# Row maximum of a 32 x 512 x 1024 array: two blocks of rows become one long block and a last row in two halves

## The chip, the cores and the metric

The kernel runs on one core of a Trainium2 chip. The metric is device time in microseconds. Before the change it is 165.11 us, the median of three runs (165.09 to 165.19).

Four parts of the core take part. The SyncE queue (SP) issues the loads, VectorE (DVE) reduces, the ScalarE queue (ACT) issues the stores, and 16 DMA engines move the bytes of both queues. TensorE does nothing.

## The reference

The input is `x`, 32 x 512 x 1024 numbers of 4 bytes, 67.11 MB. The output is the maximum over the last axis, 16,384 numbers.

```python
def reference(x: np.ndarray) -> np.ndarray:
    return np.max(x, axis=-1).astype(np.float32)
```

Every byte of `x` has to be read once and compared once; almost nothing is written.

## The kernel before, in words

The first two axes are flattened to 16,384 rows of 1024 numbers. With 128 partitions that makes 128 rows per partition.

The rows are cut into two blocks. In the first block, 112 x 128 rows, partition p holds rows 112p to 112p + 111; in the second, 16 x 128 rows, it holds 16 rows in the same way. A load takes some rows of every partition, 4 KB each, and these lie next to each other in memory within a partition. The list `BLOCKS` (line 13) gives the rows per partition of each load: it begins with loads of 14 and ends with loads of 1, 15 loads in the first block and 11 in the second.

The loads go into `ring`, a buffer of 46 rows per partition. A load takes the next free rows, and starts again at row 0 when it would run past the end. Line 49 issues the load on the SP queue. Line 50 has VectorE reduce it, with one maximum per row written to its column of `res` (128 partitions x 128 columns). After each block, line 54 issues a store of the block's columns on the ACT queue. A partition's results are adjacent in the output: pieces of 448 bytes in the first block and of 64 bytes in the second.

The framework adds the waits. A reduce waits for its load; a load waits until the reduces of the rows that it overwrites are done, and until the semaphore that it is to use is free, of which there are eight for all transfers; a store waits for its block's last reduce. Each queue issues in its own order, so what waits at its head holds up what is behind it. There is no planner with costs or due times.

Of the kernel before, what the change touches and what calls it, by code (L numbers as in the profile page):

```python
# [1 line left out]

# [4 lines left out]


F32 = mybir.dt.float32

BLOCKS = [
    [14, 14, 12, 11, 9, 8, 8, 7, 6, 5, 4, 4, 4, 3, 3],
    [2, 2, 2, 2, 2, 1, 1, 1, 1, 1, 1],
]
RING = 46


@with_exitstack  # L20
def kernel(
    ctx: ExitStack,
    tc: tile.TileContext,
    x: bass.AP,
    out: bass.AP,
):
    nc = tc.nc
    P = 128
    X = mybir.AxisListType.X

    xf = x.flatten_outer_dims()
    N, D = xf.shape
    I = N // P
    of = out.flatten_outer_dims()

    once = ctx.enter_context(tc.tile_pool(name="once", bufs=1))
    ring = once.tile([P, RING, D], F32)
    res = once.tile([P, I], F32)

    at = first = 0  # L40
    for loads in BLOCKS:
        S = sum(loads)
        xb = xf[first * P:(first + S) * P, :].rearrange("(p i) d -> p i d", p=P)
        b = 0
        for g in loads:
            if at + g > RING:
                at = 0
            xc = ring[:, at:at + g, :]
            nc.sync.dma_start(out=xc, in_=xb[:, b:b + g, :])  # L49
            nc.vector.reduce_max(out=res[:, first + b:first + b + g], in_=xc, axis=X)  # L50
            at += g
            b += g
        dst = bass.AP(tensor=of.tensor, offset=of.offset + first * P, ap=[[S, P], [1, S]])
        nc.scalar.dma_start(out=dst, in_=res[:, first:first + S])
        first += S
    assert first == I


# [1 line left out]
_INS = ['x']  # L60
_OUTS = [((32, 512), 'float32')]


# [23 lines left out]
```

## Time and profile before

| what | value |
|---|---|
| median of the runs | 165.11 us |
| the profiled execution: time | 165.1 us |
| the profiled execution: span | 163.3 us |
| VectorE busy | 138.5 us in 26 reduces (85%) |
| VectorE idle, waiting for a load | 22.4 us in 4 waits, the first of 20.1 us |
| read from memory | 67.11 MB, 411 GB/s over the span |
| mean duration of a reduce of one row | 1208 ns |
| mean duration of a reduce of 14 rows | 15086 ns |
| last store, from issue to landing | 1.4 us |

The span is the stretch between the first and the last instruction that the profiler recorded. Times within it count from its start. A line of the profile that names a group of instructions gives the source line, the engine and the operation, then what is written and read with shapes, how often, the busy time with the mean of one in ns, and the idle time ahead of it with what ended it. The chain that ended last is followed back from the last instruction, at each step to what released it. A line of a stretch gives its length, then each engine's busy time, the clock granted to TensorE, the busy share of the 16 DMA engines and the rate in GB/s.

### The profile page before, as it was taken

What the parts mean: (1) busy time and instruction counts of PE and PEld (TensorE: products, weight loads), DVE (VectorE), ACT (ScalarE), POOL (GpSimd) and SP (SyncE); (2) the same over time, 40 slices, a digit from 0 to 9 for tenths busy, and PEclk for the clock granted to TensorE, in tenths of its full rate; (3) what the DMA queues carried; (4) which work ended last, traced back from release to release, by engine and by line L of the source; (5) the groups of instructions that cost most, each with busy time, mean ns of one, the idle gap of its engine ahead of it and who ended that gap; (6) DMA issues with size and microseconds to landing.
All of it is one profiled execution on the core that took longest, in us unless ns stands there. A gap on an engine that the chain in (4) does not pass through costs nothing.

```text
span 163.3 us, 109 instructions
## 1 busy us (share of the span) xinstructions
DVE 138.5 (85%) x26; POOL 0.2 (0%) x4
## 2 busy tenths in 40 slices
DVE  0000099969999999999999999999999999999994
POOL 0000000000000000000000000000000000000000
DMA  6999999998899897999989999999999999999980
GB/s 225 449 449 449 449 449 449 449 417 385 385 409 522 353 530 321 433 433 441 473 385 473 425 449 400 434 395 451 413 425 433 429 414 418 425 421 419 404 357 2
DMA packets 4032, 67.18 MB, mean 411 GB/s; under 512 B 704, under 2 KB 704, under 8 KB 1472
## 3 DMA queue, kind: packets, MB, share of 16 engines
q1 hardware_dynamic: 3744, 67.11, 96.4%
q10 hardware_dynamic: 288, 0.07, 0.2%
HBM read 67.11 MB, written 0.07 MB: 411 GB/s over the span
## 4 chain that ended last, share of the span: by engine, by line
DMA 57%; DVE 40%; DVEq 1%; SPq 0%; issue 0%
DMA ring<-in_x_dram 57%; DVE res L50 40%; DVEq L82 1%; SPq L49 0%
## 5 line engine op out<-in xcount | busy, mean ns | idle before, releaser
L50 DVE TENSOR_REDUCE res<-ring 128x1 f32<-128x1024 f32 (+11 forms) x26 | 138.5, 5396 | 22.4 <-DMA ring<-in_x_dram 22.4
L71 POOL MEMSET const-bfloat16-1.0<- 128x1 bf16 x1 | 0.1, 101 | 0.0
L71 POOL MEMSET const-uint8-127<- 128x1 uint8 x1 | 0.1, 101 | 0.0
L71 POOL MEMSET const-float32-0.0<- 128x1 f32 x1 | 0.1, 98 | 0.2 <-issue 0.2
L71 POOL MEMSET const-float32-1.0<- 128x1 f32 x1 | 0.1, 98 | 0.0
## 6 DMA issues: line engine op xcount, KB each, us to landing
ring<-in_x_dram SPq DMA_DIRECT2D x2, 7168.0 KB, 27.6
ring<-in_x_dram SPq DMA_DIRECT2D x2, 4096.0 KB, 31.6
ring<-in_x_dram SPq DMA_DIRECT2D x1, 6144.0 KB, 49.9
ring<-in_x_dram SPq DMA_DIRECT2D x3, 2048.0 KB, 36.8
ring<-in_x_dram SPq DMA_DIRECT2D x1, 5632.0 KB, 29.7
ring<-in_x_dram SPq DMA_DIRECT2D x5, 1024.0 KB, 24.6
ring<-in_x_dram SPq DMA_DIRECT2D x1, 4608.0 KB, 23.7
ring<-in_x_dram SPq DMA_DIRECT2D x1, 3584.0 KB, 38.4
```

The costliest lines, as they stand in the source:

```text
L50: nc.vector.reduce_max(out=res[:, first + b:first + b + g], in_=xc, axis=X)
L71: nc = _bacc.Bacc("TRN2", target_bir_lowering=False, num_devices=1)
L82: with _tile.TileContext(nc) as tc:
```

## The change

The two blocks become one long block and one last row.

- The long block has 127 rows per partition, so partition p holds rows 127p to 127p + 126. Its 27 loads have the sizes in `ROWS`. The ring holds 45 rows in place of 46.
- The last row of each partition comes from the last 128 rows of the flattened input: partition p takes row 16,256 + p. It is loaded in two halves of 512 numbers (2 KB), the first into the ring, the second into a new buffer `tail` behind a gap of 16 numbers.
- The first store now comes after both of these loads in the program. It waits for the reduce of the 127th row and writes 127 numbers (508 bytes) per partition.
- The first half's maximum is written to the number just ahead of the second half in `tail`. The second reduce runs over that number and the 512 behind it, 513 in all, and so gives the maximum of the whole row. It depends on the first reduce.
- The last store writes one number (4 bytes) per partition; the 128 numbers are adjacent in the output.

```diff
-BLOCKS = [
-    [14, 14, 12, 11, 9, 8, 8, 7, 6, 5, 4, 4, 4, 3, 3],
-    [2, 2, 2, 2, 2, 1, 1, 1, 1, 1, 1],
-]
-RING = 46
+ROWS = [14, 13, 11, 11, 9, 8, 8, 7, 6, 5, 5, 4, 4, 3, 3, 2, 2, 2, 2, 1, 1, 1, 1, 1, 1, 1, 1]
+RING = 45
+RUN = 127
...
+    H = D // 2
...
+    xr = xf[:RUN * P, :].rearrange("(p i) d -> p i d", p=P)
+    out_r = bass.AP(tensor=of.tensor, offset=of.offset, ap=[[RUN, P], [1, RUN]])
...
+        x_last = xf[RUN * P:, :]
+        out_last = bass.AP(tensor=of.tensor, offset=of.offset + RUN * P, ap=[[1, P], [1, 1]])
...
-    at = first = 0
-    for loads in BLOCKS:
-        S = sum(loads)
-        xb = xf[first * P:(first + S) * P, :].rearrange("(p i) d -> p i d", p=P)
-        b = 0
-        for g in loads:
-            if at + g > RING:
-                at = 0
-            xc = ring[:, at:at + g, :]
-            nc.sync.dma_start(out=xc, in_=xb[:, b:b + g, :])
-            nc.vector.reduce_max(out=res[:, first + b:first + b + g], in_=xc, axis=X)
-            at += g
-            b += g
-        dst = bass.AP(tensor=of.tensor, offset=of.offset + first * P, ap=[[S, P], [1, S]])
-        nc.scalar.dma_start(out=dst, in_=res[:, first:first + S])
-        first += S
+    PAD = 16
+    tail = once.tile([P, PAD + H], F32)
+
+    b = at = 0
+    for g in ROWS:
+        if at + g > RING:
+            at = 0
+        xc = ring[:, at:at + g, :]
+        nc.sync.dma_start(out=xc, in_=xr[:, b:b + g, :])
+        nc.vector.reduce_max(out=res[:, b:b + g], in_=xc, axis=X)
+        at += g
+        b += g
+
+    if at + 1 > RING:
+        at = 0
+    half = ring[:, at, :H]
+    nc.sync.dma_start(out=half, in_=x_last[:, :H])
+    nc.sync.dma_start(out=tail[:, PAD:], in_=x_last[:, H:])
+    nc.scalar.dma_start(out=out_r[:, :I - 1], in_=res[:, :I - 1])
+    nc.vector.reduce_max(out=tail[:, PAD - 1:PAD], in_=half, axis=X)
+    nc.vector.reduce_max(out=res[:, I - 1:], in_=tail[:, PAD - 1:], axis=X)
+    nc.scalar.dma_start(out=out_last, in_=res[:, I - 1:])
```

More of the change, by code (lines that the diff above doesn't have):

```diff
@@ L32 @@
     N, D = xf.shape
+    H = D // 2
     I = N // P
     of = out.flatten_outer_dims()
+    assert sum(ROWS) == I - 1 and RUN >= I - 1
+    xr = xf[:RUN * P, :].rearrange("(p i) d -> p i d", p=P)
+    out_r = bass.AP(tensor=of.tensor, offset=of.offset, ap=[[RUN, P], [1, RUN]])
+    if RUN == I:
+        x_last, out_last = xr[:, I - 1, :], out_r[:, I - 1:]
+    else:
+        x_last = xf[RUN * P:, :]
+        out_last = bass.AP(tensor=of.tensor, offset=of.offset + RUN * P, ap=[[1, P], [1, 1]])
     once = ctx.enter_context(tc.tile_pool(name="once", bufs=1))
@@ L38 @@
     res = once.tile([P, I], F32)
-    at = first = 0
-    for loads in BLOCKS:
-        S = sum(loads)
-        xb = xf[first * P:(first + S) * P, :].rearrange("(p i) d -> p i d", p=P)
-        b = 0
-        for g in loads:
-            if at + g > RING:
-                at = 0
-            xc = ring[:, at:at + g, :]
-            nc.sync.dma_start(out=xc, in_=xb[:, b:b + g, :])
-            nc.vector.reduce_max(out=res[:, first + b:first + b + g], in_=xc, axis=X)
-            at += g
-            b += g
-        dst = bass.AP(tensor=of.tensor, offset=of.offset + first * P, ap=[[S, P], [1, S]])
-        nc.scalar.dma_start(out=dst, in_=res[:, first:first + S])
-        first += S
-    assert first == I
+    PAD = 16
[18 more added lines that the diff above has]
+    nc.scalar.dma_start(out=out_last, in_=res[:, I - 1:])
 _INS = ['x']
```

## The prediction

> **What bounds the kernel now.** I read the page first: the span of the profiled execution is 163.3 us and its own time 165.1 us, so 1.8 us lie around the span. The median of the three timed runs is 165.11 us, so sums made inside this span carry over to it unchanged.
>
> ```profile
> DVE 138.5 (85%) x26; POOL 0.2 (0%) x4
> ...
> HBM read 67.11 MB, written 0.07 MB: 411 GB/s over the span
> ...
> DMA 57%; DVE 40%; DVEq 1%; SPq 0%; issue 0%
> ```
>
> Neither engine nor transfer alone is the bound: the chain that ended last swaps between the load stream and VectorE. Next I read that chain in order of time, because it gives the landings at which VectorE ran dry.
>
> ```profile
> 1.15 35.88 DMA ring<-in_x_dram
> 37.05 58.02 DVE res L50 x5
> 95.08 36.77 DMA ring<-in_x_dram
> 131.87 19.94 DMA ring<-in_x_dram
> 151.84 7.92 DVE res L50 x6
> 159.75 1.13 DVEq L82
> ```
>
> The last time VectorE waited is 151.84 us (the landing is at 151.81). From there it runs through its last two-row load and six one-row loads without a gap, and the last store follows. So the end is set by VectorE after 151.81, with the stream close behind. The groups by shape price VectorE (the number behind the bar's comma is the mean of one in ns).
>
> ```profile
> L50 DVE TENSOR_REDUCE res<-ring 128x14 f32<-128x14336 f32 x2 | 30.2, 15086 | 22.0 <-DMA ring<-in_x_dram 22.0
> L50 DVE TENSOR_REDUCE res<-ring 128x1 f32<-128x1024 f32 x6 | 6.8, 1208 | 0.0
> ```
>
> The stretches at the end show when the stream stops; the last column is GB/s.
>
> ```profile
> 157.00:158.00 1.00, 1.00 (x2) 0.00 (x0) 1.00 1.02 406
> 158.00:159.00 1.00, 1.00 (x2) 0.00 (x0) 1.00 0.71 283
> 159.00:160.00 1.00, 1.00 (x2) 0.00 (x0) 1.00 0.00 0
> ```
>
> The 16 DMA engines are full until about 158.7 us. In the timeline the last reduce runs from 159.67 for 1.21, to 160.88 us. The last load was issued at 149.90 with 9.6 us to landing, so it lands near 159.46 and waits 0.2 us for VectorE. The two stores are these (last numbers: KB, and us to landing):
>
> ```profile
> out_dram<-res ACTq DMA_DIRECT2D x1, 56.0 KB, 6.6
> out_dram<-res ACTq DMA_DIRECT2D x1, 8.0 KB, 1.4
> ```
>
> The 56 KB store went out at 142.87 into a full stream, the 8 KB store at 160.91 into an empty one. It lands at about 162.3; the remaining 1.0 us to 163.3 is the program's end.
>
> **Prices from these rows.** VectorE: (15.086 - 1.208)/13 = 1.067 us per row, and a fixed 0.14 per instruction. The six one-row reduces start 1.126 apart (159.67 against 158.54 in the timeline), so a following reduce starts 0.08 before the record of the one ahead ends; each further instruction costs 0.06. Stream: 14 rows took 37.03 - 20.09 = 16.94, and the six single rows (159.46 - 151.81)/6 = 1.275 each. That is 1.205 per row and 0.07 per load. Check: 78 rows in 11 loads from 37.03 to 131.85 would be 94.76, against 94.82. From 131.85 to 151.81, 16 rows in 7 loads would be 19.77, against 19.96: the 0.19 left over is the 56 KB store among the loads.
>
> **What the Trainium skill says.** "VectorE: DVE Perf Modes", section "The DRAIN you can't avoid": two Vector instructions in a row are not safe when the second reads what the first wrote, and need a semaphore. The trace has no such pair; it shows only the 0.08 overlap that such a wait would forbid. "DMA: Bandwidth & Descriptors", section "Specifications": transfers below 512 B are read-modify-write. Both old stores are below that (448 B and 64 B per partition), and the 8 KB one lands in 1.4 us all the same; no run here shows 4 B. The same page, "Latency and other measured facts", says that large power-of-two row pitches slow copies (4 MiB: 103 GB/s; with 4 KiB more, full rate; 512 KiB: 207). The trace has pitches of 112 and 16 rows (448 and 64 KiB), and both lie on the one line of 1.205 and 0.07.
>
> **The change part by part.**
>
> 1. Loads: 26 become 27 and two halves. Rows stay 128. Three more loads cost 3 x 0.07 = +0.21. The store leaves the stream: -0.15 to -0.19. The last landing moves by about +0.05, to 159.51. A half costs 0.60 + 0.07 = 0.67, so the 127th row lands at 158.17 and the first half at 158.84. Bounds for a half, unseen before: 0.60 (bytes alone) and 1.28 (pieces of 2 KB as dear as pieces of 4 KB). I take 0.67, as the line fits pieces from 4 KB to 56 KB.
>
> 2. The smaller ring, 45 rows, and the new sizes move the waits of SP, which precede each load. Walked through with the prices above, each load still goes out more than 7 us before its bytes are needed, as now (8.7 is the shortest time to landing). SP issues two more loads at 0.33 to 0.44 each, hidden behind the 8 loads in flight. The second load has 13 rows and lands near 35.8, so VectorE's wait of 1.85 at 37.05 shrinks to about 0.65. That saves nothing: the stream makes VectorE wait again at the fourth (62.5), seventh (92.8) and thirteenth (130.6) load. SP no longer waits for the first store (5.0 in the waits of its queue); that wait was covered by loads in flight, so zero.
>
> 3. VectorE at the end. From the thirteenth load, landed near 130.6, it has 25 rows in 14 instructions before the 127th row: 25 x 1.067 + 14 x 0.06 = 27.5, so it would be free at 158.15. The row lands at 158.17: a tie, start 158.19, end 159.40. First half: already there, so it starts at 159.32 and takes 0.53 + 0.14 = 0.675, to 159.99. Second half (513 elements): it waits for the first one's result, so the overlap is lost and a release of 0.03 is added (ScalarE's store was issued at 160.91, 0.03 after 160.88). It runs from 160.02 to 160.70. Before: 160.88. So -0.18. The bounds of the wait are 0.02 and 0.15 (a second wait instruction ahead of it; the page's semaphore steps take 17 to 28 ns). Nothing is queued behind the second half but the last store.
>
> 4. The big store (128 x 508 B) is issued at about 159.43 by ScalarE, free since the start. It waits for the 127th row's reduce, and queued behind it is the last store. The stream's bytes end about 158.8, and the short store took 1.4 in an empty stream, so it lands near 160.9 to 161.2. The last store lands later, so its cost is zero. Without this cover it would need to be 1.0 us slower to show.
>
> 5. The last store: 128 pieces of 4 B side by side in place of 128 of 64 B. The packets of the old one lie in 0.2 of its 1.4 us, so even free bytes gain at most 0.1. On the other side, small writes into the same 512 B may queue up: I bound this by doubling the time, +1.4. I take +0.10.
>
> Sum: -0.18 + 0.10 = -0.08, and 165.1 - 0.08 = 165.02. I round to 165.05, because a tie at 158.17 lets small delays of either side add.
>
> **The rivals.** About 0.2% (0.33 us) is what a measurement of this kernel can tell from no change.
>
> (a) Slower: the 4 B store. Place: after 160.73, with nothing beside it. From +0.5 us in its landing the kernel is slower; at half the upper bound, +0.7 in place of +0.10, the time is 165.65. For it: the read-modify-write sentence and one shared 512 B target. Against: 64 B pieces, also small, land in 1.4.
>
> (b) The halves don't stream: each costs 1.28. The last lands at 158.17 + 2.56 = 160.73, VectorE ends at 161.43, +0.55 on before: 165.75 with the store. Against: the straight line of the stream's prices.
>
> (c) A wait takes the overlap's place: the second half writes its column of `res` only after the big store has read it. It would start at about 160.9 and end at 161.6: 165.9. Against: the reduces of the second block ran on at 142.9 to 149 with the first store in flight, so columns of `res` are kept apart.
>
> (d) The pitch of 508 KiB slows the stream by 1%: 1.4 us, 166.5. Against: two other pitches on one line, and the skill's own 4 KiB offset at full rate.
>
> (e) Faster: the store costs the stream more than its 0.19, the chained wait nothing, and the 4 B store lands 0.1 sooner; the row lands 0.15 earlier and the time is 164.65. VectorE cannot start the 127th row before it lands, which caps the gain.
>
> **How the numbers follow.** Likeliest 0.52, with its own range of 164.8 to 165.4; (a) 0.17; (b) 0.08; (c) 0.06; (d) 0.06; (e) 0.11. Slower is (a) to (d), 0.37. The range reaches up through (a), (b) and (c) to 166.1, leaving out (d) and the far end of (a), and down to 164.7, where half of (e) is out.
>
> **What would show it.** The profile after should have the last reduce starting 0.03 after the one ahead of it ends, not 0.08 before; the 127th row's reduce starting near 158.2 with at most a tenth of waiting; the DMA engines full to about 158.8; a 4 B-piece store of 0.5 KB landing in about 1.5 us; a store of 63.5 KB landing earlier than that one. I am wrong in step 5 if the last store takes 2 us or more, in step 1 if the halves land over 0.8 apart, in step 3 if VectorE reaches the 127th row late.

## The result, and the profile after

The changed kernel takes 171.11 us (median of six runs, 170.73 to 171.65), against 165.10 for the kernel before: 1.0364 times as long, 95% interval 1.0346 to 1.0382. That is 6.0 us slower. I had forecast 165.05, and a range that ended at 166.1.

The page of the kernel after, first lines, rate and chain:

```profile
span 169.4 us, 117 instructions
...
DVE 138.9 (82%) x29; POOL 0.2 (0%) x4
...
HBM read 67.11 MB, written 0.07 MB: 397 GB/s over the span
...
DVE 55%; DMA 39%; SPq 0%; issue 0%
```

VectorE is busy 0.4 us longer than before, and the rate over the span has fallen only because the span has grown. The chain in order of time, its last six pieces (start, length, what):

```profile
62.31 30.76 DMA ring<-in_x_dram
93.07 0.02 issue
93.09 66.58 DVE res L56 x21
159.67 0.60 DVE tail L66
160.28 0.02 issue
160.30 0.69 DVE res L67
```

This is where a reader can be misled. The chain names VectorE and ends at 160.30 + 0.69 = 160.99 us, but the span ends at 169.4. Before, the same chain ended at 160.88 in a span of 163.3. So 8.4 us lie behind the chain's end, against 2.4 before: 6.0 of the 6.1 us by which the span grew are there, after the last computation. What is active there stands under the transfers (KB, us from issue to landing) and in the waits of SP's queue:

```profile
out_dram<-res ACTq DMA_DIRECT2D x1, 63.5 KB, 2.3
out_dram<-res ACTq DMA_DIRECT2D x1, 0.5 KB, 7.5
```

```profile
SPq L94 <- DMA out_dram<-res: 8.7, 2, 6.5
```

The store of 0.5 KB, issued at 161.02, takes 7.5 us to land; before, a store of 8 KB took 1.4. The program's end (line 94) waits for it, 6.5 us in the longest piece. The stretch from 160 us to the end, in 40 slices of 0.235 us, shows that the DMA engines are not busy meanwhile:

```profile
GB/s 0 0 110 167 0 0 0 0 2 0 0 0 0 0 0 0 0 0 0 0 0 0 0 0 0 0 0 0 0 0 0 0 0 0 0 0 0 0 0 0
```

The big store passes in the third and fourth slice and the small one in the ninth, near 162.0. Then the engines record nothing for over 6 us. The packets have gone out, and what is still missing are the store's 16 completions: in the records they come one by one, from 3.1 to 7.5 us after the issue. Of a store that lands in 1.4 us (the first experiment below) all 16 come between 1.24 and 1.41 us.

### The profile page after: what moved, and what is told of

Read it like the earlier page. It is cut to its first block, busy times and chain, and to the rows that moved or that the text cites. A ratio compares the mean times of both kernels' runs of the same rounds, so it can differ in the third digit from the quotient of the medians.

```text
span 169.4 us, 117 instructions
## 1 busy us (share of the span) xinstructions
DVE 138.9 (82%) x29; POOL 0.2 (0%) x4
## 4 chain that ended last, share of the span: by engine, by line
DVE 55%; DMA 39%; SPq 0%; issue 0%
DVE res L56 55%; DMA ring<-in_x_dram 39%; SPq L55 0%; DVE res L67 0%; DVE tail L66 0%
## 5 line engine op out<-in xcount | busy, mean ns | idle before, releaser
L67 DVE TENSOR_REDUCE res<-tail 128x1 f32<-128x513 f32 x1 | 0.7, 689 | 0.0
L66 DVE TENSOR_REDUCE tail<-ring 128x1 f32<-128x512 f32 x1 | 0.7, 676 | 0.0
```

Source lines behind the costliest of these rows:

```text
L66: nc.vector.reduce_max(out=tail[:, PAD - 1:PAD], in_=half, axis=X)
L67: nc.vector.reduce_max(out=res[:, I - 1:], in_=tail[:, PAD - 1:], axis=X)
```

## The experiments

Three theories: **S**, small writes that fall into the same short stretch of memory pass one after another; **B**, a piece of 4 bytes is dear wherever it goes; **W**, the last store waits behind the big one just ahead of it. Beside them stood the question what the halves, the long block and the moved first store do on their own.

### The pieces of 4 bytes, moved apart

First by a long block of 128 rows, in which each partition's last row follows its other 127:

```diff
-RUN = 127
+RUN = 128
```

> The long block holds 128 rows per partition in place of 127, so the last store still writes 128 pieces of 4 bytes, but 512 bytes apart and not side by side; the halves and the order of the stores stay. Theory S (writes that fall into the same small stretch of memory pass one after another): the last store lands in about 1.5 us, not 7.5, and the time is 164.9 to 165.3. Theory B (a piece of 4 bytes is dear wherever it goes): it still lands in about 7.5 us, time about 171. Theory W (the last store waits behind the writes of the 63.5 KB store just ahead of it): about 7.5 us too. If the load pitch of 512 KiB slows the stream, the last load lands after 159.8 us, and the time is above 165.5 with a short store.

Measured: 165.51 us, ratio to before 1.0023 (1.0015 to 1.0030). The transfers of this kernel:

```profile
out_dram<-res ACTq DMA_DIRECT2D x1, 63.5 KB, 1.6
out_dram<-res ACTq DMA_DIRECT2D x1, 0.5 KB, 1.4
```

The same 128 pieces of 4 bytes, right behind the same 63.5 KB store, land in 1.4 us, and 5.6 of the 6.0 us are gone. Theories B and W fall. This kernel is 0.4 above before, which the store does not explain.

Then in the changed kernel by the address of the last store alone, 16 numbers (64 bytes) from piece to piece in a buffer of its own:

```diff
-        out_last = bass.AP(tensor=of.tensor, offset=of.offset + RUN * P, ap=[[1, P], [1, 1]])
+        aside = nc.dram_tensor("aside", [P * 16], F32).ap()
+        out_last = bass.AP(tensor=aside.tensor, offset=aside.offset, ap=[[16, P], [1, 1]])
```

> The changed kernel with the last store sent to a separate buffer in memory, where its 128 pieces of 4 bytes lie 64 bytes apart; so the last row's maxima are missing from the output. Theory S: lands in 1.4 to 2 us, time about 165. Theory B: 7.5 us, time about 171. A form of S with a wider stretch (512 bytes, eight pieces in each) would give about 0.9 + 0.6 + 8/128 of 6 us, so 1.8 to 2.5 us.

Measured: 165.43 us in one run, and in its transfers

```profile
aside<-res ACTq DMA_DIRECT2D x1, 0.5 KB, 1.5
```

Here the loads and the big store are exactly those of the change, so the address of the last store alone carries 5.7 us. 64 bytes from piece to piece are enough.

### How long is the shared stretch?

The same edit with 4 and with 8 numbers in place of 16 from piece to piece.

> The last store goes to a separate buffer with its 128 pieces of 4 bytes 16 bytes apart (the last row's maxima are missing from the output). Four pieces share 64 bytes in place of 16. If the extra 6.1 us grow with the pieces per 64 bytes: 6.1 x 3/15 = 1.2 more than the short store, so 2.6 us to landing, time about 166.6. If the line is 32 bytes, with two pieces each in place of 8: 6.1/7 = 0.9, 2.3 us. If the number of pieces alone counts: 7.5 us.

> As the run with 16 bytes, with pieces 32 bytes apart: two in each 64 bytes. If the shared stretch is 64 bytes: 6.1/15 = 0.4 more, 1.8 us to landing, time about 165.8; if it is 32 bytes or less: 1.4 to 1.5 us, as with 64 bytes apart, time about 165.4.

Measured: 165.68 and 165.70 us, one run each. The last store of the two, 16 bytes apart first:

```profile
aside<-res ACTq DMA_DIRECT2D x1, 0.5 KB, 2.2
```

```profile
aside<-res ACTq DMA_DIRECT2D x1, 0.5 KB, 1.8
```

At 32 bytes the store is 0.3 us above the 1.5 at 64 bytes. In the seven profiles whose last stores share no stretch they land in 1.4 to 1.5 us, so two pieces 32 bytes apart do seem to disturb each other; a stretch of 32 bytes or less, for which I had written 1.4 to 1.5, does not fit. At 16 bytes, four to a stretch of 64, it is 2.2. The rule of three that gave me 2.6 was not met; the 2.2 alone is nearer to the 2.3 that I had written for 32 bytes. So a stretch of about 64 bytes fits best, but its exact size rests on one execution each. Pieces side by side were not tried in the separate buffer, so the 7.5 us and these runs also differ in the buffer.

### How many pieces side by side?

The changed kernel, with its last store cut to 16, 32 or 64 partitions (here 16):

```diff
-    nc.scalar.dma_start(out=out_last, in_=res[:, I - 1:])
+    few = bass.AP(tensor=of.tensor, offset=of.offset + RUN * P, ap=[[1, 16], [1, 1]])
+    nc.scalar.dma_start(out=few, in_=res[:16, I - 1:])
```

> The changed kernel with its last store cut to the first 16 partitions: 16 pieces of 4 bytes side by side, 64 bytes in all; the other 112 maxima of the last rows are missing from the output. If the pieces that share one stretch of 64 bytes pass one after another and stretches go side by side, 16 pieces in one stretch take as long as now: about 7 us to landing, time about 170.8. If all pieces of the store pass one after another (0.05 us each, 128 of them), 16 take 0.8: about 2.2 us to landing, time about 166.

> The same with the first 32 partitions: 32 pieces, 128 bytes; the other 96 maxima are missing. Side by side lines: near 7.5 us to landing. Growth with the number: 1.4 + 1.5 = 2.9 us. Growth with the square, or nothing before an engine has several pieces in one line: 1.4 to 1.8 us.

> The changed kernel with its last store cut to the first 64 partitions: 64 pieces of 4 bytes side by side, 256 bytes; the other 64 maxima of the last rows are missing. If each 64 bytes is a line of its own with 16 pieces and lines go side by side: still near 7.5 us to landing. If the extra grows with the number of pieces: 6.1/2 = 3.0, so 4.4 us to landing, time about 168. If it grows with the square: 1.5, so 2.9 us.

Measured: 165.44, 166.79 and 170.28 us, one run each. The last store with 16, 32 and 64 pieces:

```profile
out_dram<-res ACTq DMA_DIRECT2D x1, 0.1 KB, 1.3
```

```profile
out_dram<-res ACTq DMA_DIRECT2D x1, 0.1 KB, 3.0
```

```profile
out_dram<-res ACTq DMA_DIRECT2D x1, 0.2 KB, 6.7
```

With the 7.5 us of all 128 no single one of the laws that I had written fits all four. It is neither in proportion to the number (64 pieces cost nearly as much as 128) nor the same for every full stretch (all four cases put 16 pieces into each 64 bytes, and the first costs nothing extra). Going from 64 to 128 pieces doubles the stretches and adds only 0.8 us, which would fit stretches that largely go side by side. (With 64 pieces the issue itself took 0.52 us in place of 0.34, so counted from its end it is 1.0.) What the four cases also differ in is how many pieces each DMA engine carries: every one of these stores ends in 16 completions, as many as there are engines, so if the pieces are shared out evenly it is 1, 2, 4 and 8. In the records of the 32 pieces nine of the 16 completions come by 1.30 us after the issue, as in the run with 16, and the other seven in steps, at 1.72, 2.14, 2.58 and 3.0. So in this run one more turn costs about 0.43 us, far more than the 0.05 per piece of my serial theory. It is not a price for every case: with the pieces 16 bytes apart the late completions follow each other by about 0.14.

What remains open is the law itself, and with it why 16 pieces share a stretch at no cost. That writes arriving together are merged would fit, but is only argued. A store of all 128 pieces side by side, with neighbouring pieces spread over different engines, would tell; it was not tried.

### The halves

The kernel before, with its last one-row load in two chained halves and nothing else:

```diff
...
+            if first + b == I - 1:
+                half = ring[:, at, :H]
+                x_last = xb[:, b, :]
+                nc.sync.dma_start(out=half, in_=x_last[:, :H])
+                nc.sync.dma_start(out=tail[:, PAD:], in_=x_last[:, H:])
+                nc.vector.reduce_max(out=tail[:, PAD - 1:PAD], in_=half, axis=X)
+                nc.vector.reduce_max(out=res[:, I - 1:], in_=tail[:, PAD - 1:], axis=X)
...
```

> The kernel before with one part of the change alone: its last one-row load comes in two halves, chained as in the change; both blocks and both stores stay (64 bytes per partition in the last). My step 3: VectorE ends 0.1 to 0.2 us earlier than before, time 164.9 to 165.05. The rival, that the lost overlap and the extra load eat the gain: 165.05 to 165.3. All theories on the store: the last store lands in 1.4 us.

Measured: 165.35 us, ratio 1.0016 (1.0008 to 1.0023): the halves cost 0.26 us. Its timeline at the end (start, length):

```profile
156.34 3.46 DVE L61 TENSOR_REDUCE res<-ring 128x1 f32<-128x1024 f32 x3
159.71 0.68 DVE L56 TENSOR_REDUCE tail<-ring 128x1 f32<-128x512 f32 x1
160.43 0.69 DVE L57 TENSOR_REDUCE res<-tail 128x1 f32<-128x513 f32 x1
```

VectorE is behind the loads and never idle here, so an earlier half cannot help; only the number of instructions counts. The last row takes 160.43 + 0.69 - 159.71 = 1.41 us, against 1.21 whole. That is 0.20 of the 0.26: the second half starts 0.03 to 0.04 after the end of the first, where unchained reduces overlap by 0.08, and the fixed part of a reduce is paid twice.

The opposite edit, on the changed kernel: the last row whole, with both stores as in the change.

```diff
-    half = ring[:, at, :H]
-    nc.sync.dma_start(out=half, in_=x_last[:, :H])
-    nc.sync.dma_start(out=tail[:, PAD:], in_=x_last[:, H:])
+    last = ring[:, at, :]
+    nc.sync.dma_start(out=last, in_=x_last)
     nc.scalar.dma_start(out=out_r[:, :I - 1], in_=res[:, :I - 1])
-    nc.vector.reduce_max(out=tail[:, PAD - 1:PAD], in_=half, axis=X)
-    nc.vector.reduce_max(out=res[:, I - 1:], in_=tail[:, PAD - 1:], axis=X)
+    nc.vector.reduce_max(out=res[:, I - 1:], in_=last, axis=X)
```

> The changed kernel with the last row loaded and reduced whole, in place of two halves; the stores stay (4 bytes side by side). If the stores carry the loss, the time stays at 171.0 to 171.4 and the last store at 7.5 us to landing. If the halves carry it (their chained wait, or pieces of 2 KB), it falls to about 165.1 to 165.5.

Measured: 170.85 us (170.68 to 171.24). The loss stays: its last store takes 7.2 us. The median is 0.26 below the change, but the two kernels' runs overlap, and part of it may be this store, which landed 0.3 sooner. Its first and its last reduce:

```profile
20.13 15.09 DVE L56 TENSOR_REDUCE res<-ring 128x14 f32<-128x14336 f32 x1 [20.13 <-DMA ring<-in_x_dram]
159.47 1.22 DVE L65 TENSOR_REDUCE res<-ring 128x1 f32<-128x1024 f32 x1
```

VectorE ends at 160.69, 140.56 us after its start. In the change it ends at 160.99, 140.63 after its start at 20.36. So here the halves cost no more than 0.07 by the profile.

### The long block, and the first store

The kernel before, with 128 neighbouring rows per partition in place of two blocks:

```diff
-        xb = xf[first * P:(first + S) * P, :].rearrange("(p i) d -> p i d", p=P)
+        xb = xf.rearrange("(p i) d -> p i d", p=P)[:, first:first + S, :]
...
-        dst = bass.AP(tensor=of.tensor, offset=of.offset + first * P, ap=[[S, P], [1, S]])
+        dst = bass.AP(tensor=of.tensor, offset=of.offset + first, ap=[[I, P], [1, S]])
```

> The kernel before with one edit: a partition holds 128 neighbouring rows in place of 112 and 16 (pitch 512 KiB); the same loads, reduces and moments of the stores, whose pieces of 448 and 64 bytes now lie 512 bytes apart. If the long pitch makes the first load land late (20.3 to 20.7 in six of eight profiles with 127 or 128 rows, 20.09 and 20.21 in two with 112): 165.3 to 165.6, first landing 20.3 to 20.7. If that scatter has another cause: 165.0 to 165.2.

Measured: 165.57 us, ratio 1.0032 (1.0022 to 1.0042): 0.46 us for the long pitch of loads and stores together. The chain in order of time:

```profile
1.15 36.16 DMA ring<-in_x_dram
37.31 0.02 issue
37.33 58.02 DVE res L50 x5
95.35 0.02 issue
95.37 36.75 DMA ring<-in_x_dram
132.12 0.02 issue
```

The second load lands at 37.31, against 37.03 before, and the thirteenth at 132.12, against 131.85. From one to the other it is 94.81 us, and 94.82 before. So the stream's rate is untouched; the delay that this profile shows arises at the start and is hardly made up. The first reduce, which follows the first landing, shows it; the line of before comes second:

```profile
20.41 15.09 DVE L50 TENSOR_REDUCE res<-ring 128x14 f32<-128x14336 f32 x1 [20.41 <-DMA ring<-in_x_dram]
```

```profile
20.11 15.09 DVE L50 TENSOR_REDUCE res<-ring 128x14 f32<-128x14336 f32 x1 [20.11 <-DMA ring<-in_x_dram]
```

In the eleven profiles with blocks of 127 or 128 rows it starts at 20.13 to 20.75; in the three with 112 rows, at 20.11, 20.23 and 20.24. The two groups overlap. The profile shows 0.3 of the 0.46, and a single profile scatters by as much; so that the whole 0.46 lies at the start is likely, but not shown. Why the start is slower was not separated either.

Both repairs together, the last row whole and the pieces 512 bytes apart:

> The changed kernel without the two parts that cost: 128 rows per partition in the long block, so that the last store's pieces of 4 bytes lie 512 bytes apart, and the last row whole. By the earlier runs: the halves cost 0.26 (171.11 against 170.85), so 165.51 - 0.26 = 165.25 if the load list of the change gives nothing; VectorE of the whole-row kernel ended at 160.69, against 160.88 before, so with a last store of 1.4 us: 165.1 - 0.2 = 164.9. Faster than before if below 164.9, same if 164.95 to 165.25.

Measured: 165.44 us, ratio 1.0026 (1.0015 to 1.0038). I had hoped for 164.9 to 165.25. Its first reduce starts at 20.64, against 20.11 before, so what the load list gives, the late start takes.

The first store of the kernel before, issued by SP behind the last load:

```diff
-        nc.scalar.dma_start(out=dst, in_=res[:, first:first + S])
+        if first + S == I:
+            nc.sync.dma_start(out=early, in_=res[:, :first])
+            nc.scalar.dma_start(out=dst, in_=res[:, first:first + S])
+        early = dst
```

> The kernel before with its 56 KB store issued by SP behind the last load, so that its packets queue behind the loads and not among them; all else stays, the last store's 64-byte pieces too. If the store costs the stream 0.14 to 0.19 and VectorE follows the stream: VectorE ends near 160.72 in place of 160.88, time 164.93 to 165.0. If that cost is covered: 165.1. If the store now holds up the end: it lands after 162.3, time above 165.2.

Measured: 165.03 us, ratio 0.9995 (0.9987 to 1.0003). It cannot be told from before; the interval leaves room for a gain of 0.2 us at most. In its profile VectorE's last reduce begins at 159.60 in place of 159.67, although its first load landed 0.12 later, so the 0.15 to 0.19 that I had priced for the store is not refuted either. No kernel here beats the one before beyond its interval.

## Why the prediction was wrong

**Step 5 failed, in size.** I priced the last store at +0.10 with an upper end of +1.4; it measured 7.5 - 1.4 = +6.1. Rival (a) named the place and the kind of cost, but carried only +0.7 and 165.65, and the range ended at 166.1, below even the upper end of +1.4. That upper end had no measurement behind it: I doubled a row that had no two pieces in one 64-byte stretch. Pieces of 64 bytes side by side fill one stretch each; pieces of 4 bytes put 16 writes into it. What the row of before bounds is a store without sharing, and such a store of 4-byte pieces does take 1.4 to 1.5 us. The Trainium skill's sentence on read-modify-write ("DMA: Bandwidth & Descriptors", section "Specifications") is not the price by itself: pieces of 4, 64 and 508 bytes are all below its 512, and they landed in 1.4, 1.4 and 1.6 us where no two of them shared 64 bytes. Whether the dear step is such a read-modify-write, no run here shows; that the addresses carry the cost is shown, how the writes to one stretch are passed stays open.

**Step 3 had the end of VectorE's work right, but not its start.** These are the first reduce and that of the 127th row in the profile after:

```profile
20.36 15.09 DVE L56 TENSOR_REDUCE res<-ring 128x14 f32<-128x14336 f32 x1 [20.36 <-DMA ring<-in_x_dram]
158.45 1.22 DVE L56 TENSOR_REDUCE res<-ring 128x1 f32<-128x1024 f32 x1
```

The 127th row's reduce began at 158.45 in place of 158.19, 0.02 after the row landed, and VectorE ended at 160.99 in place of 160.70. From there to the end I had 2.51 and it took 2.54, the chained wait 0.03 as forecast. The missing 0.26 was there from the first landing (20.36 against 20.11). I had also not seen where the gain of 0.18 came from. By my own prices a whole last row lands at 158.17 + 1.275 = 159.45 and VectorE ends at 160.68, no later than the 160.70 of the halves. So the halves gain nothing; what gains is the load list and the store out of the stream, and the run with the whole row ended at 160.69.

**Step 1 held.** In the records the two halves land 0.68 and 0.63 us after the load ahead of each (158.43, 159.11, 159.74), for a forecast of 0.67. Rival (b) is out.

**Step 2 held.** VectorE waited at 36.09 (0.65 us), 62.75 and 93.09, as walked through. At the thirteenth load no idle time stands in the profile, but its reduce began at 130.89, 0.02 after the landing, so it did wait there, by less than the overlap of two reduces.

**Step 4 held with less room.** The big store took 2.3 us, to 162.0, where I had 160.9 to 161.2. A last store of 1.4 would still have landed later, at 162.4. Its pieces of 508 bytes adjoin, so nearly all neighbours share the 64 bytes where they meet; laid so, this store took 1.8 to 2.3 us in eight profiles, and 1.6 in the two with 512 bytes from piece to piece. That fits the same sharing on a small scale, but was not tested alone.

**Rival (c)** is out: the second half began 0.03 after the end of the first, with the big store in flight. **Rival (d)** was right in a form I had not written: with 128 rows the long pitch costs 0.46, and none of it in the rate, on which my argument against it rested. The 127 rows of the change were not measured alone; its profile starts 0.25 later than before. **Rival (e)** is out: the store moved out of the stream gains 0.2 at most.

The sum, from the profiles before and after: the last store is issued at 161.02 in place of 160.91, +0.11, and takes 6.1 longer; together 6.2, for a span longer by 6.1 and a time longer by 6.0. The 0.11 is made up of three small terms: the first landing is 0.25 later, the load list with the moved store gives 0.21 (140.77 us from VectorE's start to its end before, 140.56 with the whole row), and the halves take 0.07 of that back. Each of the three rests on single profiles.

## What to carry to other kernels

Before splitting a result so that each partition stores one number, look where the numbers lie in memory: here 128 pieces of 4 bytes landed in 1.4 to 1.5 us when they were 64 bytes or more apart and in 7.5 when they were adjacent. A store after the last computation has no cover, so its worst case belongs in the range, and a measured store bounds another only if it has the same neighbours. When the chain that ended last stops well short of the span's end, read the landing times of the transfers and the waits of the queue that ends the program.

## What the runs showed that I had not expected

Adjacent pieces of 4 bytes: 16 landed in 1.3 us, 32 in 3.0, 64 in 6.7 and 128 in 7.5. The DMA engines' records were empty for the last 6 us of it. A row pitch of 512 KiB left the stream's rate as it was (94.81 us for the same loads) and the kernel was still 0.46 us slower; its profile shows 0.3 of that, as a later first landing. Splitting the last row into chained halves cost 0.26 us where VectorE was behind the loads.
